# Retention head 0: score products moved behind the fifth of the seven value/gate products, and half of one product sum moved to the other transposition bank

## The chip, the cores and the metric

The kernel runs on one core of one Trainium2 chip, as a single launch. The metric is the device time in microseconds (us), the median of three executions. Beside it there is one profiled execution, whose trace gives the start and length of every instruction on each engine: PE (TensorE, matrix products and transposes), DVE (VectorE), ACT (ScalarE), POOL (GpSimd), SP (the engine that issues most of the loads) and the DMA queues. Each engine runs its instructions strictly in the order in which they stand in its own list; between engines they wait for one another by semaphores.

## What is computed

A two-layer encoder on 512 tokens of width 1024, float32. Layer one is latent attention beside a pooling mixer; it is not touched. Layer two is bidirectional retention with four heads (query and key width 256, value width 512). Cut to what matters:

```python
h = rms_norm(x, norm_g)
q, k, v, gate = jnp.split(h @ w_in, [RET_QK, 2 * RET_QK, 2 * RET_QK + RET_V], axis=-1)
q = apply_rope(q.reshape(B_, T, RET_HEADS, RET_DK), cos_r, sin_r)
k = apply_rope(k.reshape(B_, T, RET_HEADS, RET_DK), cos_r, sin_r) * (RET_DK ** -0.5)
o = o_f + o_b            # retention forward and backward: (q k^T * decay) v, all 512 x 512 pairs here
o = (o - mu) * lax.rsqrt(var + NORM_EPS) * gn_g     # norm per head
y = o * jax.nn.silu(gate)
x = x + y @ w_out
```

The kernel holds the 512 x 512 decay factors of a head as shifted views of one table `gp` and so computes each head in one pass: scores, times decay, times values.

## The kernel before

**Arithmetic.** Every float32 operand is split in a high part (rounded for the fast matmul, a CAST on ACT, names ending in H) and a low remainder (a subtraction on DVE, names ending in L). A product of two such operands is three matmuls: H with H, L with H, H with L. In `mm3` these are lines 72, 75 and 76, in the products of `vg` lines 792, 794 and 795. One matmul is 128 x 128 against 128 x 512.

**Head 0 of layer two, in program order.** `qk_gemm` and `rope_pair` make q and k (rotation: lines 768 to 773 on DVE, split: lines 81 and 82). The inverse norms of the tokens come from a small chain: `ss2` on DVE (line 1005), scale and epsilon on DVE (line 175), a power on POOL (line 177), then three small copies on DVE (lines 1006 to 1008: `r2`, `nr2`, `r2s`). `decay(h)` fills `gp` (lines 731 and 732 on DVE, an exponential on ACT, line 733). `r_scores` makes four 128 x 512 score tiles in PSUM, six matmuls each, two buffers named `sc`; each is scaled and multiplied by the decay on DVE (line 864) and split (lines 81 and 82). `vg` makes the values and the gate. `r_head_out` then multiplies scores by values (48 matmuls), multiplies by the gate and turns the result with PE transposes into the two PSUM buffers named `tr` (`turn`, line 877).

**The seven products of `vg`.** Values and gates of a head are one 2 x 2 block product, done in Strassen's way with seven products of half size instead of eight. In order they are A11, S1, S4, S2, S3, A12, A22, 24 matmuls each (two weight tiles i = 0, 1, each for two token halves p = 0, 1). They are summed in PSUM in three pairs of tiles, X, Z and Y, one tile for each half p: A11 and A12 go to X, S1 and S4 to Z, S2, S3 and A22 to Y. Before a later product may add to a pair, DVE has read the intermediate sum: line 826 reads Z after S1, lines 835 and 836 read Y after S2 and Z after S4, line 842 reads Y after S3, line 851 after A22. ACT copies X after A11 to SBUF (line 821, `p1`), which lines 826, 835 and 851 add.

**Weights.** A weight tile is 128 x 1024. ACT casts it (line 784, `wH`, four buffers), DVE subtracts (line 785, `wL`, three buffers). Raw tiles arrive in four `raw` buffers by SP loads (line 682) of 512 KB. The pair `t3` for S3 is a load followed by an adding DMA issued from POOL (line 684) to the same buffer; POOL's power of line 177 stands ahead of the two adding DMAs in POOL's list. The pair `b21` is loaded to the two `raw` buffers in which `b22` lies, so each of its loads waits until DVE has made the `wL` of that `b22` tile (product S4). Line 829 adds `b22` and line 839 adds `b21` to the pair `tt`, which is the weight of S1, then of S2, then of A22.

**What sets the order.** A scheduler of the language layer reorders the instructions of each engine when the program is built, except where one is held in program order (`keep_in_program_order`, which `mm3` takes as its `pin`). So the order on an engine isn't the text's, but it is fixed before the run.

Of the kernel before, what the change touches and what calls it, by code (L numbers as in the profile page):

```python
# [37 lines left out]
def trunk(ctx: ExitStack, tc: tile.TileContext, x, positions, a_norm_g, a_w_in, a_q_norm_g, a_w_uq,  # L38
# [11 lines left out]
    def S(tag, shape=(P, T), dt=F32):  # L50
        count[0] += 1
        return sb.tile(list(shape), dt, tag=tag, name=f"{tag}_{count[0]}", bufs=BUFS[tag])
# [4 lines left out]
    def PS(tag):  # L57
        count[0] += 1
        return ps.tile([P, T], F32, tag=tag, name=f"{tag}_{count[0]}", bufs=PBUFS[tag])

    mm = nc.tensor.matmul
# [6 lines left out]
    def f(ap):  # L68
        return ap.bitcast(F32)

    def mm3(pt, lH, lL, rH, rL, st, sp, pin=False):
        i = mm(pt, lhsT=lH, rhs=rH, start=st, stop=False)  # L72
        if pin:
            tc.keep_in_program_order(i)
        mm(pt, lhsT=lH, rhs=rL, start=False, stop=False)  # L75
        mm(pt, lhsT=lL, rhs=rH, start=False, stop=sp)  # L76

    def split(src, tag):
        h = S(tag, dt=F32R)
        l = S(tag, dt=F32R)  # L80
        nc.scalar.copy(h, src)
        V.tensor_sub(l, src, f(h))
        return h, l
# [255 lines left out]
    ss = S("sm", (P, 4))  # L339
# [166 lines left out]
    def values(g4):  # L506
        uH, uL = wunit(ukv[:, g4 * 4:(g4 + 1) * 4, 128:256], 4, P)
        uH = uH.rearrange("p a b -> p (a b)")
        uL = uL.rearrange("p a b -> p (a b)")
        vH, vL = [], []  # L510
        for t in range(4):
            pt = PS("mm")
            tk = slice(t * P, (t + 1) * P)
            mm3(pt, kvH[:, tk], kvL[:, tk], uH, uL, True, True)
            h, l = split(pt, "V")
            vH.append(h)
            vL.append(l)
        return vH, vL
# [79 lines left out]
    vv = values(0)  # L598
# [5 lines left out]
    for h in range(8):  # L604
# [3 lines left out]
        if h == 4:  # L608
            vv = values(1)
# [65 lines left out]
    def vg_src(h, r, c, i):  # L675
        c0 = 4096 - c * 2048 + h * T
        return wv[:, r, 2 * i:2 * i + 2, c0:c0 + T]
# [9 lines left out]
    def first_sums(h, then=lambda i: i):  # L687
        return [load("tw", vg_src(h, 0, 0, i), vg_src(h, 0, 1, i), then=then) for i in range(2)]

    tt0 = first_sums(0, pin)  # L690
# [38 lines left out]
    def decay(h):  # L729
        e = gp.rearrange("p a b -> p (a b)")[:, :E]  # L730
        V.tensor_scalar(out=e, in0=idx, scalar1=nlb[:, 4 + h:5 + h], scalar2=1.0, op0=ALU.mult, op1=ALU.mult)
        V.scalar_tensor_tensor(out=e, in0=idx, scalar=lg[:, h:h + 1], in1=e, op0=ALU.mult, op1=ALU.min)
        act(e, e, AF.Exp)
        return [e[:, (3 - j) * P:(3 - j) * P + T] for j in range(4)]
# [38 lines left out]
        V.tensor_add(c, c, d)  # L773
        return split(a, tag), split(c, tag)

    def vg(h, tt=None):

        tags = dict(X=("mm", "mm"), Z=("mm", "tr"), Y=("mm", "sc"))
        ps_ = {n: [PS(t) for t in tt] for n, tt in tags.items()}

        def product(name, a, ws, first):
            for i in range(2):
                wh, wl = S("wH", (P, 1024), F32R), S("wL", (P, 1024), F32R)
                nc.scalar.copy(wh, ws[i])  # L784
                V.tensor_sub(wl, ws[i], f(wh))  # L785
                last = i == 1
                for p in range(2):
                    o = ps_[a][p]
                    for k2 in range(2):
                        c = slice(k2 * T, (k2 + 1) * T)  # L790
                        lh, ll = (x[:, p * P:(p + 1) * P] for x in forms[2 * i + k2][name])
                        mm(o, lhsT=lh, rhs=wh[:, c], start=first and i == 0 and k2 == 0, stop=False,  # L792
                           skip_group_check=True)
                        mm(o, lhsT=lh, rhs=wl[:, c], start=False, stop=False, skip_group_check=True)  # L794
                        mm(o, lhsT=ll, rhs=wh[:, c], start=False, stop=last and k2 == 1, skip_group_check=True)  # L795

        vv = [None] * 4
        gs = [None] * 4

        def value(t, src):  # L800
            sm = S("sm", (P, 4))
            act(src, src, AF.Copy, scale=nr2[:, t:t + 1], accum_out=sm[:, 0:1])
            V.tensor_scalar(out=sm[:, 1:2], in0=sm[:, 0:1], scalar1=-1.0 / T, scalar2=1.0, op0=ALU.mult, op1=ALU.mult)
            hh = S("V", dt=F32R)
            ll = S("V", dt=F32R)
            act(hh, src, AF.Identity, bias=sm[:, 1:2])
            V.scalar_tensor_tensor(out=ll, in0=src, scalar=sm[:, 1:2], in1=f(hh), op0=ALU.add, op1=ALU.subtract)
            vv[t] = (hh, ll)

        rng = range(2)  # L810

        def src(r, c, i):
            return vg_src(h, r, c, i)

        b11 = [load("raw", src(0, 0, i)) for i in rng]
        if tt is None:
            tt = first_sums(h)
        product("A11", "X", b11, True)
        p1 = [S("t") for _ in rng]
        for p in rng:  # L820
            nc.scalar.copy(p1[p], ps_["X"][p])
        b22 = [load("raw", src(1, 1, i)) for i in rng]
        product("S1", "Z", tt, True)
        v = [S("t") for _ in rng]
        for p in rng:
            V.tensor_add(v[p], ps_["Z"][p], p1[p])
        t3 = [load("raw", src(0, 1, i), src(1, 1, i), then=pin) for i in rng]
        for i in rng:
            V.tensor_add(tt[i], tt[i], b22[i])
        product("S4", "Z", b22, False)  # L830
        b21 = [load("raw", src(1, 0, i)) for i in rng]
        product("S2", "Y", tt, True)
        u2 = [S("t") for _ in rng]
        for p in rng:
            V.tensor_add(u2[p], ps_["Y"][p], p1[p])
            V.tensor_add(u2[p], ps_["Z"][p], u2[p])
            value(p, u2[p])
        for i in rng:
            V.tensor_add(tt[i], tt[i], b21[i])
        product("S3", "Y", t3, False)  # L840
        for p in rng:
            V.tensor_add(v[p], ps_["Y"][p], v[p])
            value(2 + p, v[p])
        product("A12", "X", b21, False)
        for p in rng:
            gs[p] = S("l1")
            act(gs[p], ps_["X"][p], AF.Silu, scale=r2[:, p:p + 1])
        product("A22", "Y", tt, False)
        for p in rng:
            c = S("l1")  # L850
            V.tensor_add(c, ps_["Y"][p], p1[p])
            act(c, c, AF.Silu, scale=r2[:, 2 + p:3 + p])
            gs[2 + p] = c
        return vv, gs

    def r_scores(q, k, ds, tag):
        ss = []
        for j in range(4):
            tk = slice(j * P, (j + 1) * P)
            pt = PS("sc")  # L860
            for i in range(2):
                mm3(pt, k[i][0][:, tk], k[i][1][:, tk], q[i][0], q[i][1], i == 0, i == 1)
            s = S("t")
            V.scalar_tensor_tensor(out=s, in0=pt, scalar=r2s[:, j:j + 1], in1=ds[j], op0=ALU.mult, op1=ALU.mult)
            ss.append(split(s, tag))
        return ss
# [116 lines left out]
    for h in range(4):  # L983
        A, B = ("qk", "y") if h % 2 == 0 else ("y", "qk")
        if h == 0:
            res = [residual(0), residual(1)]
            next(res[0])
            pq = qk_gemm(0, 1)
            sums_of_halves(0)
            sums_of_halves(1)  # L990
            next(res[0])
            pq += qk_gemm(P, 1)
            pk = qk_gemm(1024, 1)
            sums_of_halves(2)
            sums_of_halves(3)
            next(res[1])
            next(res[1])
        else:
            pq = qk_gemm(h * 256, then=pend[2])
            pk = qk_gemm(1024 + h * 256, 1)  # L1000
            rs = out_scale(pend[1])
        q = rope_pair(pq, A)
        k = rope_pair(pk + qk_gemm(1024 + h * 256 + P, 1), A)
        if h == 0:
            V.tensor_add(ss2[:, 0:4], ss2[:, 0:4], ss2[:, 4:8])
            V.tensor_copy(r2, pow_mhalf(ss2[:, 0:4], 1.0 / DM))
            V.tensor_scalar(out=nr2, in0=r2, scalar1=-1.0, scalar2=1.0, op0=ALU.mult, op1=ALU.mult)
            V.tensor_scalar(out=r2s, in0=r2, scalar1=0.0625, scalar2=1.0, op0=ALU.mult, op1=ALU.mult)
        else:
            r_out(h - 1, pend[0], rs)  # L1010
        ss = r_scores(q, k, decay(h), B)
        vv, gs = vg(h, tt0 if h == 0 else None)
        pend = r_head_out(ss, vv, gs, A)
    for i in range(2):
        gt = S("y" if A == "qk" else "qk")
# [47 lines left out]
```

## Time and profile before

| | |
|---|---|
| runs | 792.81 us median of 3 (792.67, 792.81, 794.54) |
| profiled execution | 794.41 us, of which 792.6 us span from first to last instruction |
| PE busy | 781.1 us, 99% of the span, mean granted clock 0.998 |
| DVE busy | 579.0 us (73%) |
| ACT busy | 403.4 us (51%) |
| POOL busy | 38.6 us (5%) |
| DMA | 80.91 MB, mean 102 GB/s |

The "span" is the time between the first and the last instruction of the profiled execution. A row of the timeline has the start, the length, the engine, the line, the operation, the tiles written and read, and in square brackets how long the engine had been idle just before and who released it. A matmul row's length is its whole passage through the array; matmuls that don't wait start 0.227 us apart although each is shown as 0.39 us long. In head 0 the products lie between 403 and 451 us.

### The profile page before, as it was taken

How to read it: one execution, taken by the hardware profiler on the slowest of the kernel's cores; microseconds unless marked ns; L12 is line 12 of the kernel's file. 1: busy time of each engine (PE TensorE's matmuls, PEld its weight loads, DVE VectorE, ACT ScalarE, POOL GpSimd, SP SyncE). 2: the span in 40 equal slices, each digit the busy share in tenths (PEclk: the TensorE clock that was granted, in tenths of full speed). 3: DMA queues.
4: the chain of work that ended last, by engine and by line, in shares of the span. 5: the costliest groups of instructions: out<-in, count | busy, mean ns of one | idle time of the engine just before them, and what ended most of it. 6: DMA issues, size and time to landing. Idle time of an engine off the chain costs nothing. (4 is left out here: it accounts for less than half of the span.)

```text
span 792.6 us, 9592 instructions
## 1 busy us (share of the span) xinstructions
PE 781.1 (99%) x3546; PEld 642.0 (81%) x3546; DVE 579.0 (73%) x938; ACT 403.4 (51%) x670; POOL 38.6 (5%) x60
## 2 busy tenths in 40 slices
PE   9999999999999999999999999999999999999996
PEld 7888888888888888888877888888888888888885
DVE  4689986768748677899679747787377884767845
ACT  6645346666626744318654832358333583334832
POOL 0010000000000000100010100100101001010003
PEclk9999999999999999999999999999999999999999
DMA  8722233132123312353315822447324373244202
GB/s 254 226 62 83 70 82 87 39 80 91 54 72 88 103 38 69 87 152 107 107 37 133 227 56 80 111 111 210 74 79 110 103 203 84 71 122 102 85 27 108
DMA packets 87832, 80.91 MB, mean 102 GB/s; under 512 B 7868, under 2 KB 67304, under 8 KB 87784
## 3 DMA queue, kind: packets, MB, share of 16 engines
q1 hardware_dynamic: 82984, 71.11, 29.8%
q0 software_dynamic: 4352, 8.39, 7.0%
q10 hardware_dynamic: 448, 0.79, 0.3%
q8 instruction: 28, 0.46, 0.2%
q14 instruction: 20, 0.16, 0.1%
HBM read 76.87 MB, written 2.10 MB: 100 GB/s over the span
## 5 line engine op out<-in xcount | busy, mean ns | idle before, releaser
L72 PE MATMUL mm<-hT,wH 128*128 128x512 f32 x352 | 139.0, 395 | 0.3 <-ACT wH L281 0.3
L75 PE MATMUL mm<-hT,wH 128*128 128x512 f32 x352 | 137.8, 392 | 0.0
L76 PE MATMUL mm<-hT,wL 128*128 128x512 f32 x352 | 137.8, 392 | 0.0
L108 ACT CAST wH<-raw 128x1024 fp32r<-128x1024 f32 (+3 forms) x77 | 70.7, 923 | 114.4 <-PE mm L75 91.3
L109 DVE TENSOR_TENSOR wL<-raw,wH 128x1024 fp32r<-128x1024 f32 (+3 forms) x77 | 81.4, 1059 | 13.1 <-issue 4.7
L72 PEld LDWEIGHTS mm<-hT,wH 128*128 128x128 f32 x352 | 66.5, 189 | 14.0 <-ACT wH L281 0.7
L76 PEld LDWEIGHTS mm<-hT,wL 128*128 128x128 f32 x352 | 66.5, 189 | 14.0 <-DVE wL L282 0.2
L75 PEld LDWEIGHTS mm<-hT,wH 128*128 128x128 f32 x352 | 66.5, 189 | 13.6
L784 ACT CAST wH<-raw 128x1024 fp32r<-128x1024 f32 x32 | 33.7, 1054 | 50.2 <-PE mm L76 20.2
L785 DVE TENSOR_TENSOR wL<-raw,wH 128x1024 fp32r<-128x1024 f32 x32 | 38.9, 1220 | 10.4 <-issue 7.2
L784 ACT CAST wH<-tw 128x1024 fp32r<-128x1024 f32 x24 | 25.1, 1047 | 40.9 <-PE mm L76 26.3
L904 ACT ACTIVATE wH<-raw,cols 128x512 fp32r<-128x512 f32 x32 | 21.4, 717 | 43.8 <-issue 32.8
L925 DVE SCALAR_TENSOR_TENSOR xT<-mm,sm,xT 128x512 f32<-128x512 f32 (+1 forms) x33 | 24.1, 731 | 25.1 <-PE mm L76 25.0
L75 PE MATMUL mm<-y,wH 128*128 128x512 f32 x96 | 37.2, 389 | 0.0
L76 PE MATMUL mm<-y,wL 128*128 128x512 f32 x96 | 37.2, 389 | 0.0
L72 PE MATMUL mm<-y,wH 128*128 128x512 f32 x96 | 37.2, 390 | 0.0
L785 DVE TENSOR_TENSOR wL<-tw,wH 128x1024 fp32r<-128x1024 f32 x24 | 29.3, 1220 | 2.8 <-PE tr L794 1.0
L794 PE MATMUL mm<-wL,hT 128*128 128x512 f32 x80 | 31.1, 389 | 0.0
L795 PE MATMUL mm<-wH,hT 128*128 128x512 f32 x80 | 31.1, 389 | 0.0
L792 PE MATMUL mm<-wH,hT 128*128 128x512 f32 x80 | 31.0, 389 | 0.0
L885 DVE TENSOR_TENSOR l<-mm,l 128x512 f32<-128x512 f32 x16 | 11.1, 692 | 23.9 <-PE mm L76 23.9
L504 DVE TENSOR_TENSOR xT<-mm,xT 128x512 f32<-128x512 f32 x24 | 16.4, 688 | 15.0 <-PE mm L76 14.8
(361 smaller groups left out, 1903.6 us busy)
## 6 DMA issues: line engine op xcount, KB each, us to landing
raw<-in_r_w_in_dram SPq DMA_DIRECT2D x48, 512.0 KB, 3.7
raw<-in_a_w_in_dram SPq DMA_DIRECT2D x25, 512.0 KB, 4.0
raw<-in_a_w_out_dram SPq DMA_DIRECT2D x16, 512.0 KB, 3.9
raw<-in_r_w_out_dram SPq DMA_DIRECT2D x16, 512.0 KB, 5.5
tw<-in_r_w_in_dram SPq DMA_DIRECT2D x8, 512.0 KB, 3.8
tw<-in_r_w_in_dram POOLq DMA_DIRECT2D x8, 512.0 KB, 6.6
raw<-in_r_w_in_dram POOLq DMA_DIRECT2D x8, 512.0 KB, 6.0
l<-in_x_dram SPq DMA_DIRECT2D x8, 256.0 KB, 4.7
```

The source lines that it names most:

```text
L72: i = mm(pt, lhsT=lH, rhs=rH, start=st, stop=False)
L75: mm(pt, lhsT=lH, rhs=rL, start=False, stop=False)
L76: mm(pt, lhsT=lL, rhs=rH, start=False, stop=sp)
L108: then(nc.scalar.copy(h[:, c], raw[:, c]))
L109: then(V.tensor_sub(l[:, c], raw[:, c], f(h[:, c])))
L784: nc.scalar.copy(wh, ws[i])
L785: V.tensor_sub(wl, ws[i], f(wh))
L792: mm(o, lhsT=lh, rhs=wh[:, c], start=first and i == 0 and k2 == 0, stop=False, skip_group_check=True)
L794: mm(o, lhsT=lh, rhs=wl[:, c], start=False, stop=False, skip_group_check=True)
L795: mm(o, lhsT=ll, rhs=wh[:, c], start=False, stop=last and k2 == 1, skip_group_check=True)
L904: act(wh[:, c], raw[:, c], AF.Copy, scale=g)
L925: V.scalar_tensor_tensor(out=a, in0=pt[:, :T // n], scalar=rs[:, t:t + 1], in1=a, op0=ALU.mult, op1=ALU.add)
```

## The change

For head 0 alone, `r_scores` is no longer called ahead of `vg` but by `vg` itself, behind S3 and its two value tiles and ahead of A12; `decay(0)` is called there too. For all four heads the second tile of the pair Y is taken from the `tr` buffers instead of the `sc` buffers. The very first score matmul of each head is held in program order.

```diff
-    def vg(h, tt=None):
-
-        tags = dict(X=("mm", "mm"), Z=("mm", "tr"), Y=("mm", "sc"))
+    def vg(h, tt=None, mid=None):
+
+        tags = dict(X=("mm", "mm"), Z=("mm", "tr"), Y=("mm", "tr"))
         ps_ = {n: [PS(t) for t in tt] for n, tt in tags.items()}
...
             V.tensor_add(v[p], ps_["Y"][p], v[p])
             value(2 + p, v[p])
+        if mid:
+            mid()
         product("A12", "X", b21, False)
...
-                mm3(pt, k[i][0][:, tk], k[i][1][:, tk], q[i][0], q[i][1], i == 0, i == 1)
+                mm3(pt, k[i][0][:, tk], k[i][1][:, tk], q[i][0], q[i][1], i == 0, i == 1, i == 0 and j == 0)
...
-        ss = r_scores(q, k, decay(h), B)
-        vv, gs = vg(h, tt0 if h == 0 else None)
+        if h == 0:
+            ss = []
+            vv, gs = vg(h, tt0, lambda: ss.extend(r_scores(q, k, decay(0), B)))
+        else:
+            ss = r_scores(q, k, decay(h), B)
+            vv, gs = vg(h)
```

What the scheduler makes of it shows in the order of the instructions. In its rows a tile's name carries a running number, and the numbers of the same tile differ between the two kernels: Z is `mm_3919` and `tr_3920` before and `mm_3864` and `tr_3865` now; the line numbers of the changed file are 2 higher behind line 843.

PE, at the start of S1, before (`qk_3797` and `qk_3798` are q, `qk_3846` is k, `sc` tiles are scores):

```order
L795 MATMUL mm_3918<-wH_3943,hT_3528 128x512
L792 MATMUL mm_3919<-wH_3967,pt_3611 128x512
L792 MATMUL tr_3920<-wH_3967,pt_3611 128x512
L72 MATMUL sc_3865<-qk_3797,qk_3846 128x512
L75 MATMUL sc_3865<-qk_3798,qk_3846 128x512
L72 MATMUL sc_3878<-qk_3797,qk_3846 128x512
L75 MATMUL sc_3878<-qk_3798,qk_3846 128x512
L794 MATMUL mm_3919<-wL_3968,pt_3611 128x512
L795 MATMUL mm_3919<-wH_3967,pt_3612 128x512
L792 MATMUL mm_3919<-wH_3967,pt_3629 128x512
```

The same place now:

```order
L795 MATMUL mm_3863<-wH_3888,hT_3528 128x512
L792 MATMUL mm_3864<-wH_3912,pt_3611 128x512
L792 MATMUL tr_3865<-wH_3912,pt_3611 128x512
L794 MATMUL mm_3864<-wL_3913,pt_3611 128x512
L795 MATMUL mm_3864<-wH_3912,pt_3612 128x512
L792 MATMUL mm_3864<-wH_3912,pt_3629 128x512
```

Before, all 24 score matmuls stood inside S1, 12 in the half of each weight tile; now S1's matmuls follow each other, and the first that needs a `wL` stands directly behind the two that don't. The scores now stand behind S3: 12, then 3 of A12, then 12.

ACT, over the same stretch, before (`t_3959` and `t_3960` are `p1`, the copies of X):

```order
L784 CAST wH_4011<-raw_3963 128x1024
L784 CAST wH_4027<-raw_3965 128x1024
L81 CAST qk_3846<-t_3836 128x512
L81 CAST qk_3850<-t_3838 128x512
L784 CAST wH_4047<-tw_3375 128x1024
```

and now:

```order
L784 CAST wH_3956<-raw_3908 128x1024
L821 COPY t_3904<-mm_3862 128x512
L821 COPY t_3905<-mm_3863 128x512
L784 CAST wH_3972<-raw_3910 128x1024
L81 CAST qk_3846<-t_3836 128x512
L81 CAST qk_3850<-t_3838 128x512
L784 CAST wH_3992<-tw_3375 128x1024
```

The two copies of X have moved from behind the score splits to a place ahead of the second `b22` cast and the splits of k.

DVE, from the reads of Z after S1 to the read of Y after S2, before (`tw` is `tt`; `wL_4102` and `wL_4118` are the two tiles of `t3` for S3):

```order
L785 TENSOR_TENSOR wL_4064<-tw_3378,wH_4063 128x1024
L731 TENSOR_SCALAR gp<-l_783_3371,nlb 128x896
L839 TENSOR_TENSOR tw_3375<-tw_3375,raw_4043 128x1024
L839 TENSOR_TENSOR tw_3378<-tw_3378,raw_4045 128x1024
L785 TENSOR_TENSOR wL_4102<-raw_4003,wH_4101 128x1024
L785 TENSOR_TENSOR wL_4118<-raw_4006,wH_4117 128x1024
L732 SCALAR_TENSOR_TENSOR gp<-l_783_3371,lg,gp 128x896
L835 TENSOR_TENSOR t_4079<-mm_3921,t_3959 128x512
```

and now:

```order
L785 TENSOR_TENSOR wL_3957<-raw_3908,wH_3956 128x1024
L785 TENSOR_TENSOR wL_3973<-raw_3910,wH_3972 128x1024
L785 TENSOR_TENSOR wL_3993<-tw_3375,wH_3992 128x1024
L785 TENSOR_TENSOR wL_4009<-tw_3378,wH_4008 128x1024
L839 TENSOR_TENSOR tw_3375<-tw_3375,raw_3988 128x1024
L785 TENSOR_TENSOR wL_4047<-raw_3948,wH_4046 128x1024
L839 TENSOR_TENSOR tw_3378<-tw_3378,raw_3990 128x1024
L785 TENSOR_TENSOR wL_4063<-raw_3951,wH_4062 128x1024
L835 TENSOR_TENSOR t_4024<-mm_3866,t_3904 128x512
```

The four score multiplications and their four splits, and the two lines of head 1's decay, are gone from here to behind S3; both additions of `b21` and both `wL` of `t3` still stand ahead of the first read of Y. Two loads of activation tables are new on ACT, around head 1's exponential, which now stands between the gate's first and second pair of SiLUs. The lists of SP and POOL are the same as before, and from head 1 on only the buffer name of Y's second tile differs.

## Prediction

> **What bounds the kernel now.** I read the page's engine table first, then the busy time of the engines by stretch, then PE's timeline in head 0's products.
>
> ```profile
> span 792.6 us, 9592 instructions
> PE 781.1 (99%) x3546; PEld 642.0 (81%) x3546; DVE 579.0 (73%) x938; ACT 403.4 (51%) x670; POOL 38.6 (5%) x60
> ...
> 409.00:424.00 15.00, 12.46 (x52) 9.49 (x52) 13.91 (x23) 7.04 (x11) 3.81 (x3) 1.00 0.45 67
> 424.00:435.00 11.00, 10.54 (x47) 8.35 (x46) 10.18 (x11) 3.85 (x4) 0.00 (x0) 1.00 0.47 143
> ```
>
> PE is the bound of the whole. The two stretches (length, then busy us of PE, PEld, DVE, ACT, POOL) are an exception: PE has gaps, and DVE is 93% busy in both, so here DVE paces PE. The timeline of PE has the gaps in place.
>
> ```profile
> 403.06 0.39 PE L792 MATMUL mm<-wH,hT 128*128 128x512 f32 x1
> ...
> 408.73 0.39 PE L792 MATMUL tr<-wH,pt 128*128 128x512 f32 x1
> 410.32 0.50 PE L72 MATMUL sc<-qk,qk 128*128 128x512 f32 x1 [1.20 <-ACT qk L81]
> 410.66 0.39 PE L75 MATMUL sc<-qk,qk 128*128 128x512 f32 x1
> ...
> 421.45 0.45 PE L792 MATMUL mm<-wH,l 128*128 128x512 f32 x1
> 422.61 0.49 PE L792 MATMUL tr<-wH,l 128*128 128x512 f32 x1 [0.71 <-DVE t L826]
> 423.74 0.50 PE L794 MATMUL mm<-wL,l 128*128 128x512 f32 x1 [0.64 <-DVE wL L785]
> 434.94 0.50 PE L792 MATMUL mm<-wH,l 128*128 128x512 f32 x1 [0.46 <-DVE t L835]
> 450.96 0.39 PE L72 MATMUL mm<-V,y 128*128 128x512 f32 x1
> ```
>
> The four waits in brackets are 3.0 us together; a change that neither adds nor removes a matmul can win little more than these. From 403.06 to 408.73 are 25 steps, 0.227 us each; after a wait the first step is 0.34 (410.32 to 410.66), 0.11 lost again.
>
> **The equal-time point.** The row at 434.94 is the first matmul of S3; 450.96 is the first of `r_head_out`. Before, 70 matmuls lie from the one to the other; now it is 96, the 24 scores and 2 of A12 more. With 0.227 a step and 0.11 for the restart, S3 would have to begin at 450.96 - 0.11 - 96 x 0.227 = 429.1 for the same time. The change is therefore worth (start of S3) - 429.1, if nothing waits behind it.
>
> **PE's own way to S3.** These rows carry it.
>
> ```profile
> 408.70 1.05 ACT L784 CAST wH<-raw 128x1024 fp32r<-128x1024 f32 x1 [1.66 <-PE mm L795]
> 409.66 1.14 ACT L81 CAST qk<-t 128x512 fp32r<-128x512 f32 x2
> ...
> 419.45 1.07 ACT L821 COPY t<-mm 128x512 f32<-128x512 f32 x2
> 408.92 1.22 DVE L785 TENSOR_TENSOR wL<-tw,wH 128x1024 fp32r<-128x1024 f32 x1
> 410.30 0.69 DVE L82 TENSOR_TENSOR qk<-t,qk 128x512 fp32r<-128x512 f32 x1 [0.16 <-ACT qk L81]
> ...
> 412.60 0.17 DVE L1006 COPY r<-sm 128x4 f32<-128x4 f32 x1 [0.93 <-POOL sm L177]
> 412.67 1.23 DVE L785 TENSOR_TENSOR wL<-tw,wH 128x1024 fp32r<-128x1024 f32 x1
> ...
> 421.87 0.68 DVE L826 TENSOR_TENSOR t<-tr,t 128x512 f32<-128x512 f32 x1
> 422.47 2.35 DVE L785 TENSOR_TENSOR wL<-raw,wH 128x1024 fp32r<-128x1024 f32 x2
> ```
>
> *First wait.* The scores no longer stand at 408.96, but the first L794 of S1 does, and its `wL` is made from 408.92 to 410.14. PE starts 0.06 behind a DVE end (422.55, 422.61): 410.20, 1.24 lost where 1.36 was. The wait changes its name only.
>
> *Second wait, new.* The copies of X now stand ahead of the second cast on ACT. The second needs A11's last matmul, which released the cast at 408.70; so copy 408.70, cast 409.23, split of k 410.19 instead of 409.66: 0.53 later, and with it, through L82, the norm's chain and POOL's power, everything from 412.60 on DVE. The second `wL` of S1 ends at 412.67 + 0.53 + 1.23 = 414.43. PE, with no scores between, wants it at 410.20 + 0.34 + 10 x 0.227 = 412.81: 1.68 lost. Queued behind it are S1's rest and all later products.
>
> *S4.* DVE steps on by 1.14 for a 1024 wide row (the x2 row), 0.60 for a 512 wide one (421.87 to 422.47) and 0.07 for a small one (412.60 to 412.67): two small copies, two L829, two L826, the second ending at 418.04, then the first `wL` of S4, ending at 419.18. PE wants S4's second matmul at 417.78 and, after 0.227, its first L794: it loses 0.32 and 0.90, where 0.93 (421.45 to 422.61) and 0.90 (to 423.74) were. The eight score operations are no longer in DVE's way, but PE lacks the 5.4 us of score matmuls too.
>
> Together, with a restart of 0.11 behind each of three, 1.24 + 1.68 + 0.32 + 0.90 + 0.33 = 4.5 us are lost, against 3.5 up to here before (1.36 + 0.93 + 0.90 + 0.33). From 408.73, 70 matmuls: PE reaches S3 at 408.96 + 15.9 + 4.5 = 429.3.
>
> **DVE's and the DMAs' way to S3.** S3's first matmul waits for L835, and ahead of that stand the two L839 and both `wL` of `t3`.
>
> ```profile
> 411.16 1.40 POOL L177 TENSOR_TENSOR sm<-sm,mhalf 128x4 f32<-128x4 f32 x1 [72.41 <-DVE sm L175]
> 412.53 1.23 POOL L684 DMA_DIRECT2D raw<-in_r_w_in_dram  x1
> 418.89 1.22 POOL L684 DMA_DIRECT2D raw<-in_r_w_in_dram  x1 [5.13 <-issue]
> 423.76 1.52 SPq L682 DMA_DIRECT2D raw<-in_r_w_in_dram  x2
> DMA to landing us min/median/max: 6.0/6.0/6.0
> ...
> DMA to landing us min/median/max: 8.6/8.6/8.6
> DMA to landing us min/median/max: 9.0/9.0/9.0
> ...
> DMA to landing us min/median/max: 6.1/6.3/7.8
> ```
>
> The first landing line is POOL's adding DMAs at 410 to 420 us, alone on the DMA engines; the next two are POOL's at 545.7 and 645.5, while SP's loads run; the last is SP's loads in the former's company. Before, the second adding DMA (418.89 to 424.9) was over when SP issued the loads of `b21` (423.76, 0.07 behind the first `wL` of S4, and one `wL` later). Now that `wL` is done at 419.18, so SP issues at 419.25 and 420.38, and POOL's DMA, late by the 0.53 of the power, at 419.42. They collide. By the collision's rows the adding DMA lands at 419.42 + 8.6 to 9.0 = 428.0 to 428.4, the second load at 420.38 + 6.1 to 7.8 = 426.5 to 428.2. Behind the adding DMA come its cast (1.05), its `wL` (1.14 to the next on DVE), L835 (0.68) and two handovers (0.08): S3 at 431.0 to 431.4. The load's own way (L839 1.14, `wL` 1.14, L835 0.74) ends no later. So S3 begins 1.9 to 2.3 us behind the equal-time point, 2.1 in the middle, and PE, there since 429.3, waits.
>
> A rule of the Trainium skill bears on this (DMA: Bandwidth & Descriptors, "Queues, rings and completion order"): each DMA engine goes round between the queues that have work, packet by packet. If instead the older request were served first, the adding DMA would keep its 6.0 and land at 425.4; the sum would then be set by PE's own way, +0.2. The trace agrees with the rule: 8.6 and 9.0 against 6.0.
>
> **Behind S3.** Scores: 24 matmuls, four multiplications, four casts and four subtractions move; they issue no DMA. The multiplications take
>
> ```profile
> L864 DVE SCALAR_TENSOR_TENSOR t<-sc,r2s,gp x16: 739/743/749, 415.1 to 714.0; 128x512 f32<-128x512 f32 x16
> ```
>
> 0.74 each. DVE's next `wL` needs the buffer that S3's last L794 gives back, 22 steps and 0.39 after S3's start, 5.5 us; behind it come that `wL` (1.14), a value step of the same kind as L864 (0.66 to the next), a small one (0.07), the read of Y (0.60) and the first score multiplication (0.74): 8.7 and a handover, 8.8. PE wants that score buffer again 39 matmuls after S3's start, at 9.0. Hidden, with 0.15 to spare; if the cover goes, each 0.1 of slip costs 0.1, at most one 0.74. Head 1's decay and two more table loads on ACT:
>
> ```profile
> 445.02 1.28 ACT L847 ACT_TABLE_LOAD   x1
> 452.14 0.68 DVE L851 TENSOR_TENSOR l<-sc,t 128x512 f32<-128x512 f32 x1
> 459.62 0.60 PE L877 MATMUL tr<-ident,l 128*128 128x128 f32 x4
> 459.82 0.69 DVE L885 TENSOR_TENSOR l<-mm,l 128x512 f32<-128x512 f32 x1 [1.46 <-PE mm L76]
> ```
>
> 2 x 1.28 on ACT ahead of the second pair of SiLUs, whose first reader is the L885 at 459.82: nothing, with some 4 us of cover; without it 2.6 at most. The Y tile in a `tr` buffer: its last read is the L851 at 452.14, the next writer of that buffer the turn at 459.62: nothing, here and in the other heads, whose order is the same. Between 0 and 0.7 in all; I take 0.
>
> **Sum.** +2.1 us. On the profiled execution's own time, 794.41 (1.8 around its 792.6 span), that is 796.5; the median of the runs is 1.6 lower, 792.81, and gives 794.9, 0.26% more. What a measurement here tells from no change is about 0.3%, 2.4 us, so this is "no change", but close to its edge.
>
> **Rivals.** *Slower: the adding DMA is starved.* Before, DVE's second addition of `b21` started when its load had landed:
>
> ```profile
> 429.73 1.23 DVE L839 TENSOR_TENSOR tw<-tw,raw 128x1024 f32<-128x1024 f32 x1 [0.59 <-DMA raw<-in_r_w_in_dram]
> ```
>
> If `b21` goes first (before, 6.0 us from SP's issue at 423.76 until L839 could start at 429.73; now to 425.2) and the adding DMA's 6.0 less its 1.23 of issue follows, it lands at 430.0; halfway between that and the forecast's 428.4 is 429.2, S3 at 432.2, +3.1 us, 795.9. It decides from a landing later than 428.5, 9.1 us after its issue: then the loss passes 2.4. For it: 9.0 has been seen. Against: 8.6 too, and there as much load traffic ran beside it.
>
> *No collision that matters.* The adding DMA lands by 426.3, as in 6.0 to 6.9 us; then PE's own way counts, 429.3, +0.2 us, 793.0. For it: the first of the two loads has the engines to itself for its first 1.2 us or so, until POOL's packets come. Against: the three transfers start within 1.2 us of each other.
>
> *Faster: DVE's relief pays out.* DVE loses the eight score operations in the stretch, 4 x (0.66 + 0.60) = 5.0 us, PE its 5.4; in the rows before DVE was the later of the two. If all waits but the first (1.35 with its restart) went, 4.2 - 1.35 = 2.9 us would be won, 789.9. It needs the second `wL` of S1 1.7 us earlier than worked out, and the power of 1.40 us on POOL stands before it.
>
> *The clock drops.* PE would now stand still three times for 1.2 to 1.9 us.
>
> ```profile
> 6.95 0.80 PE L72 MATMUL mm<-hT,wH 128*128 128x512 f32 x1 [0.32 <-ACT wH L281]
> ...
> 10.53 0.39 PE L76 MATMUL mm<-hT,wL 128*128 128x512 f32 x1
> ```
>
> At the kernel's start 8 matmuls took 3.58 us instead of 1.82; one such stretch costs 1.8 us more, +3.9, 796.7. Against: before, waits of 1.20 and of 0.71 and 0.64 in close order left the granted clock at 1.00. The Trainium skill (TensorE: Matmul & The Clock Gate, "Why this matters for your kernels") warns of idle gaps above about 3 us; none here is so long.
>
> **Numbers.** Forecast 0.45, starved 0.28, no collision 0.20, clock 0.04, faster 0.03. The forecast's upper end lies at the bound, so a fifth of it counts as slower: slower 0.41, same 0.56, faster 0.03. The range goes from below the no-collision case (792.6) to the clock's case and the worst landing (796.7); the forecast's own is 794.3 to 795.5.
>
> **What the new trace would show.** A wait of about 1.2 us for S1's first `wL` and of 1.6 for its second, released by DVE L785; SP's loads of `b21` issued near 419.3 and 420.4; POOL's second adding DMA landing 8 to 9 us after issue; then PE idle some 1.7 us at S3's first L792, released by L835; none of size at the scores. I am wrong if `b21` or the adding DMA land early, if the scores wait for their buffers, or if a matmul step anywhere behind 409 us is 0.43.

## The result and the profile after

The changed kernel took 798.41 us (median of 6 runs, 796.68 to 799.17) against 793.94 (6 runs, 792.67 to 795.17): a ratio of 1.0052, 95% interval 1.0039 to 1.0065. It is 4.5 us slower, where 2.1 were forecast (794.9, from 792.6 to 796.7). The forecast stood on 792.81 for the kernel before; its median over six runs is 1.1 higher, so 1.1 of the 3.5 us between 794.9 and 798.41 is not the change. The profiled execution of the changed kernel took 796.9 us, 1.5 less than the median; why is told with the second group of experiments.

The engine table of the changed kernel's page:

```profile
span 795.1 us, 9592 instructions
PE 780.0 (98%) x3546; PEld 640.7 (81%) x3546; DVE 579.5 (73%) x938; ACT 406.3 (51%) x672; POOL 38.6 (5%) x60
```

TensorE is busy for 1.1 us less and idle for longer. Its waits, largest first (what waited, for what, us in total, times, longest):

```profile
PE mm L792 <- DVE t L835: 3.4, 1, 3.4
PE mm L794 <- DVE wL L785: 3.1, 3, 1.4
```

Before, the wait for L835 was 0.46 us and those for L72, L826 and `wL` were 1.20, 0.71 and 0.64. The scores now wait for nothing. The places of the waits on TensorE's timeline, from the first S1 matmul on the `tr` tile (408.73 before, 407.39 here: this execution got through the kernel's start 1.34 us sooner, mostly because the product at 7 us ran at about 0.23 us a step and not at the half clock of the prediction's rows, so its times are to be read 1.34 later against the prediction's) to the first of `r_head_out`:

```profile
407.39 0.39 PE L792 MATMUL tr<-wH,pt 128*128 128x512 f32 x1
408.85 0.50 PE L794 MATMUL mm<-wL,pt 128*128 128x512 f32 x1 [1.08 <-DVE wL L785]
413.10 0.50 PE L794 MATMUL mm<-wL,pt 128*128 128x512 f32 x1 [1.43 <-DVE wL L785]
417.84 0.50 PE L794 MATMUL mm<-wL,l 128*128 128x512 f32 x1 [0.64 <-DVE wL L785]
427.72 0.39 PE L795 MATMUL tr<-wH,pt 128*128 128x512 f32 x1
431.49 0.47 PE L792 MATMUL mm<-wH,l 128*128 128x512 f32 x1 [3.38 <-DVE t L835]
453.44 0.39 PE L72 MATMUL mm<-V,y 128*128 128x512 f32 x1
```

From the first row to the last are 46.05 us; before, from 408.73 to 450.96, 42.23. That is 3.82 us more for the same matmuls. S3's first matmul, the row at 431.49, stands 24.10 us behind the first row, and the equal-time point stood at 20.4 (429.1 - 408.73): 3.7 of the 3.82 are lost by then, most of them in the 3.38 us ahead of this row. VectorE, POOL and SP show what it waited for:

```profile
422.19 1.23 DVE L839 TENSOR_TENSOR tw<-tw,raw 128x1024 f32<-128x1024 f32 x1 [0.70 <-DMA raw<-in_r_w_in_dram]
423.33 1.22 DVE L785 TENSOR_TENSOR wL<-raw,wH 128x1024 fp32r<-128x1024 f32 x1
428.38 1.23 DVE L839 TENSOR_TENSOR tw<-tw,raw 128x1024 f32<-128x1024 f32 x1 [3.83 <-DMA raw<-in_r_w_in_dram]
429.52 1.22 DVE L785 TENSOR_TENSOR wL<-raw,wH 128x1024 fp32r<-128x1024 f32 x1
430.66 0.69 DVE L835 TENSOR_TENSOR t<-mm,t 128x512 f32<-128x512 f32 x1
...
411.67 1.23 POOL L684 DMA_DIRECT2D raw<-in_r_w_in_dram  x1
418.09 1.22 POOL L684 DMA_DIRECT2D raw<-in_r_w_in_dram  x1 [5.18 <-issue]
417.86 1.52 SPq L682 DMA_DIRECT2D raw<-in_r_w_in_dram  x2
424.58 0.37 SPq L100 DMA_DIRECT2D raw<-in_r_w_in_dram  x1
```

SP issues the two loads of `b21` within 1.2 us, the first of them 0.2 us ahead of POOL's second adding DMA. That first load is there for VectorE 4.3 us after its issue (422.19). VectorE then stands still for 3.83 us, until the second load has landed, with the addition, a `wL` and L835 in line behind it, 3.0 us of work that TensorE sits out. The adding DMA's own time from issue to landing was 6.0 us alone before; here it is

```profile
DMA to landing us min/median/max: 10.0/10.0/10.0
```

and VectorE could start on the second load, issued near 419.0, 9.4 us later. The two ways end almost together: the cast of the adding DMA's tile starts on ACT at 428.21 and ends near 429.3, and its `wL` starts at 429.52. The row at 424.58 was not in the sum: head 1's first weight load, which SP now also issues while these are in flight.

### The profile page after: what moved, and what is told of

Read it like the earlier page. It is cut to its first block, busy times and chain, and to the rows that moved or that the text cites. A ratio compares the mean times of both kernels' runs of the same rounds, so it can differ in the third digit from the quotient of the medians.

```text
span 795.1 us, 9592 instructions
## 1 busy us (share of the span) xinstructions
PE 780.0 (98%) x3546; PEld 640.7 (81%) x3546; DVE 579.5 (73%) x938; ACT 406.3 (51%) x672; POOL 38.6 (5%) x60
## 4 chain that ended last, share of the span: by engine, by line
PE 84%; issue 11%; DVE 3%; DMA 1%; POOL 1%; ACT 0%; POOLq 0%; DVEq 0%; SPq 0%
PE mm L72 18%; PE mm L76 18%; PE mm L75 18%; PE mm L792 4%; PE mm L795 4%; PE mm L794 4%; PE tr L792 2%; PE tr L795 2%; PE tr L794 2%; PE sc L72 2%; PE sc L75 2%; PE sc L76 2%; PE tr L575 2%; DMA raw<-in_r_w_in_dram 1%; PE sc L557 1%
## 5 line engine op out<-in xcount | busy, mean ns | idle before, releaser
L72 PE MATMUL mm<-hT,wH 128*128 128x512 f32 x352 | 138.2, 393 | 0.3 <-ACT wH L281 0.3
L72 PEld LDWEIGHTS mm<-hT,wH 128*128 128x128 f32 x352 | 66.1, 188 | 14.0 <-ACT wH L281 0.7
L785 DVE TENSOR_TENSOR wL<-raw,wH 128x1024 fp32r<-128x1024 f32 x32 | 39.0, 1222 | 10.4 <-issue 7.2
L72 PE MATMUL mm<-y,wH 128*128 128x512 f32 x96 | 37.2, 390 | 0.0
```

## Experiments

**First group: where does the wait come from?** The theory was the prediction's collision, harder than priced; the rivals were the moved tile of Y, and a wait that has nothing to do with the DMAs. The first kernel is the change once more.

> The changed kernel once more, beside the others on one chip. Collision theory: +3.8 us of waits in head 0 against before, 3.4 us of it one wait at S3's first matmul. Clock theory: some executions carry a second slow stretch of the clock and show 0.996 instead of 0.998 as the mean clock, 1.7 us longer; about half of them or more, so ratio 1.004 to 1.006. If the clock readings are chance and have nothing to do with the wait, before and the other kernels of this call show 0.996 just as often.

It took 798.92 us against 793.76 (ratio 1.0073, 1.0055 to 1.0092), above the expected 1.004 to 1.006; all six executions had the low clock. The waits were the same but for a longer one at S3 (3.75 us; the adding DMA took 10.4), and behind that wait this execution shows something that the changed kernel's profile had not:

```profile
432.00 0.47 PE L792 MATMUL mm<-wH,l 128*128 128x512 f32 x1 [3.75 <-DVE t L835]
432.31 0.39 PE L794 MATMUL mm<-wL,l 128*128 128x512 f32 x1
...
433.12 0.63 PE L794 MATMUL mm<-wL,l 128*128 128x512 f32 x1
433.55 0.63 PE L795 MATMUL mm<-wH,l 128*128 128x512 f32 x1
...
436.41 0.39 PE L792 MATMUL mm<-wH,l 128*128 128x512 f32 x1
```

From 433.12 the matmuls start 0.43 us apart instead of 0.227, and at 436.41 the usual step is back. More on that below.

Y's second tile in the `tr` bank alone, with the scores where they were:

```
-        tags = dict(X=("mm", "mm"), Z=("mm", "tr"), Y=("mm", "sc"))
+        tags = dict(X=("mm", "mm"), Z=("mm", "tr"), Y=("mm", "tr"))
```

> The kernel before with only the second tile of the sum Y in a transposition bank; the scores stay where they were. Collision theory: the bank is free long before it is wanted, so 0.0 us, ratio 0.999 to 1.001, clock 0.998. Rival, the bank costs by itself (a turn that waits for the last read of Y, in each of four heads): about +1 us a head, ratio 1.004 to 1.005.

Measured 794.17 us, ratio 1.0004 (0.9992 to 1.0016); the wait at S3 is 0.4 us, as before, and from the first S1 matmul on the `tr` tile to `r_head_out` are 42.22 us (42.23 before). The bank costs nothing, so the loss belongs to the order.

The change, with the second of the two adding DMAs left out in the first head:

```
-        t3 = [load("raw", src(0, 1, i), src(1, 1, i), then=pin) for i in rng]
+        t3 = [load("raw", src(0, 1, i), *([] if h == 0 and i == 1 else [src(1, 1, i)]), then=pin) for i in rng]
```

> The change, but in head 0 the second adding DMA of the pair t3 is left out (that half of the weight of S3 lacks a summand). Collision theory: the two loads of b21 are alone on the DMA engines and land 3.7 and 4.9 us after issue, S3 does not wait (under 0.3 us), ratio 1.000 to 1.001, all executions at clock 0.998. Rival, the order on DVE alone (both additions of b21 and both subtractions of t3 ahead of the read of Y): the wait at S3 stays at 2 us or more and the ratio at 1.003 or more.

Measured 793.48 us, ratio 1.0006 (0.9992 to 1.0020). TensorE's waits in it:

```profile
PE mm L794 <- DVE wL L785: 3.2, 3, 1.5
PE sc L160 <- POOL t L157: 1.3, 1, 1.3
PE mm L72 <- ACT wH L281: 0.8, 1, 0.8
```

The three waits for `wL` stand as in the change, the one at S3 is gone, and with it all of the loss, although both additions of `b21` and both `wL` of `t3` still stand ahead of the read of Y. The rest of the reordering is worth +0.2 us (42.41 from the first row to `r_head_out`, against 42.23), as the prediction's case without a collision had it. That all executions would have a clock of 0.998 did not come true: 4 of 12 had 0.994 to 0.996, and were 2.4 us and more longer than the rest.

The change, with the adding DMAs out of the loads' way: the chain of the token norms is written behind them, so that POOL does not stand at its power before it issues. `token_norm` holds the four lines of `ss2`, `r2`, `nr2` and `r2s`, taken out of the loop over heads.

```
+    def token_norm():
...
         t3 = [load("raw", src(0, 1, i), src(1, 1, i), then=pin) for i in rng]
+        if h == 0:
+            token_norm()
```

> The change, but the small chain for the token norm (with the power on POOL) stands behind the two adding DMAs of t3 in the program. POOL can then issue the adding DMAs as soon as the first loads have landed, near 398 and 404 us, so they are over before the loads of b21 start, and the second subtraction for S1 no longer waits for the power. Collision theory: no wait at S3, the second wait in S1 (1.4 us in the change) gone, the first (1.1 us) stays; worked out to S3 starting 0.9 us ahead of the equal-time point, ratio 0.998 to 1.000, clock 0.998. Rival, order on DVE: S3 still waits 2 us or more, ratio 1.003 or more.

Measured 792.38 us, ratio 0.9986 (0.9975 to 0.9998). Lines from 776 on are 6 to 8 higher in this kernel. POOL's issues on the timeline:

```profile
396.25 1.21 POOL L684 DMA_DIRECT2D raw<-in_r_w_in_dram  x1 [58.66 <-DVE wL L791]
405.30 1.22 POOL L684 DMA_DIRECT2D raw<-in_r_w_in_dram  x1 [7.84 <-DVE qk L82]
```

TensorE's waits:

```profile
PE mm L800 <- DVE wL L791: 1.7, 2, 1.0
PE sc L160 <- POOL t L157: 1.3, 1, 1.3
```

The second adding DMA now starts at 405.30 and lands in 6.2 us; `b21` is loaded from 416.82, alone; S3 waits for nothing. The new second wait (1.4) is gone too. Both kernels that keep the DMAs apart lose the wait: the collision is its cause.

**Which transfers collide?** Head 1's load at 424.58 had been left out of the sum. It was to be held back by one more tile of the `raw` ring.

```
         b21 = [load("raw", src(1, 0, i)) for i in rng]
+        if h == 0:
+            G.memset(S("raw", (P, 1024))[:, 0:1], 0.0)
```

> The change, with one more tile of the `raw` ring taken by a one-column memset on POOL behind b21's loads, so that the load of head 1's first weight tile waits for the splits of t3's second tile and no longer runs beside b21's loads and the adding DMA. If the third load is what made the landings late (the sum left it out): the adding DMA lands at most 9.2 us after its issue (10.0 in the changed kernel), b21's second load at most 8.2 (9.4), the wait at S3 falls to 1.5 to 2.5 us (3.4), the clock stretch goes with it, and the time is 794.5 to 796.0 us. Rival, b21's two loads do it alone: the adding DMA still takes 9.6 or more, S3 waits 3.2 us or more, the time is 797.5 to 799.0.

This failed as a test: the memset was over at 424.40, the ring gave its tile to the load at once, and SP issued it at 424.43, as in the change. It took 799.23 us (ratio 1.0075), one more repeat. With a second write to that tile, by VectorE behind S2's sums, the hold is real:

```
+        if h == 0:
+            hold = S("raw", (P, 1024))[:, 0:1]
+            G.memset(hold, 0.0)
...
             value(p, u2[p])
+        if h == 0:
+            V.tensor_copy(hold, u2[1][:, 0:1])
```

> The change, with a tile of the `raw` ring taken by a one-column memset on POOL behind b21's loads and written once more by VectorE behind the sums of S2, so that head 1's first weight load can't start until then (about 431 instead of 424.5). This time the load is really held. If that third load made the landings late: the adding DMA lands at most 9.2 us after its issue (10.0 to 10.3 in the changed kernel), b21's second load at most 8.2 (9.4), the wait at S3 is 1.5 to 2.5 us, no stretch at half clock, 794.0 to 795.8 us. Rival, b21's two loads do it alone: the adding DMA takes 9.6 or more, S3 waits 3.2 us or more, 797.5 to 799.2.

SP's issues in it, and S3's first matmul:

```profile
419.86 1.52 SPq L682 DMA_DIRECT2D raw<-in_r_w_in_dram  x2
432.72 0.37 SPq L100 DMA_DIRECT2D raw<-in_r_w_in_dram  x1
...
433.44 0.47 PE L792 MATMUL mm<-wH,l 128*128 128x512 f32 x1 [3.30 <-DVE t L838]
```

POOL's adding DMA, issued at 420.02:

```profile
DMA to landing us min/median/max: 10.0/10.0/10.0
```

The third load starts at 432.72, behind it all, and the adding DMA still takes 10.0 us and S3 still waits 3.30. So `b21`'s second load (9.3 here) and the adding DMA are as late without the third load; the load missing from the sum cost nothing. The time was 800.53 us, ratio 1.0083 (1.0055 to 1.0111), above even the rival's range; the profiled execution (800.44) came 2.0 us later to the first S1 matmul on the `tr` tile than the changed kernel's, of which more below.

**Second group: does the wait drop the clock?** Of the 12 executions of the change, 2 had a mean granted clock of 0.998 (796.68 and 796.90 us, one of them the profiled one) and 10 had 0.994 to 0.996 (797.97 to 801.29). Of 29 of the kernel before, 5 were at 0.995 or 0.996, and of the 34 of the three kernels above without the wait, 11 were at 0.994 to 0.996, so the wait is not the only thing that lowers it. The theory: a TensorE idle for so long is given half the clock for a while. The rival: the low clock goes with the crowded DMAs, or comes by chance. The test makes the wait without the DMAs, on the kernel with the norm moved, by n idle reads of Y's first tile on VectorE:

```
         u2 = [S("t") for _ in rng]
+        for i in range(n if h == 0 else 0):
+            V.scalar_tensor_tensor(out=v[0], in0=ps_["Y"][0], scalar=0.0, in1=v[0], op0=ALU.mult, op1=ALU.add)
```

> Base: the kernel with the norm behind the adding DMAs (e3_norm_behind_adds: 792.4 us, no wait at S3). Ahead of VectorE's reads of Y behind S2, two more reads of Y's first tile (first head only; they add zero times Y to v). No DMA is changed. Worked out from that kernel's rows (a dependent 128x512 step each 0.73 us, VectorE's read starting at 425.75 and TensorE's S3 due at 427.0): TensorE waits 1.0 us at S3. Both theories: about +1.0 us, 793.0 to 794.0, no stretch at half clock.

> As with two reads, with four, and one weight split that the scheduler puts between them: TensorE waits 3.5 us at S3, as in the changed kernel, but with no late DMA. If the wait itself drops the clock: a stretch at half clock behind S3's start in most executions, clock 0.994 to 0.996 in most runs, and 3.5 + 1.5 us over the base: 796.7 to 798.0. If the low clock came with the crowded DMAs or by chance: clock as the base (0.997 to 0.999 in 8 of 11), and 3.5 us over it: 795.4 to 796.4.

> As with two reads, with seven, and two weight splits between them: TensorE waits 6.9 us at S3. If the wait itself drops the clock: every execution has the stretch at half clock of about 3.4 us, and the time is 6.9 + 1.6 us over the base: 800.4 to 801.6. If not: clock as the base, 798.8 to 799.8.

All three missed the wait they were built for. The scheduler saw the delay and put matmuls of A12 ahead of S3, so TensorE waited at most 1.0 us anywhere there; with four reads (us in total, times, longest):

```profile
PE mm L800 <- DVE wL L791: 2.5, 3, 1.0
```

The times were 793.14, 793.99 and 796.36 us (ratios 0.9997, 1.0004 and 1.0033; the first inside its range, but with a wait of 0.3 us at S3 instead of 1.0), and with seven reads the granted clock was 0.997 to 0.999 in all six runs. They say nothing on long waits, but the profiled execution with two reads tells where a low mean can come from: its 0.996 is a stretch at half clock from 7.6 to 11.0 us, at the kernel's start, and no other until the kernel's last microseconds. With the matmuls of S2, S3 and A12 kept in the order written, the wait comes:

```
+            one = pin if h == 0 and name in ("S2", "S3", "A12") else lambda i: i
...
-                        mm(o, lhsT=lh, rhs=wl[:, c], start=False, stop=False, skip_group_check=True)
+                        one(mm(o, lhsT=lh, rhs=wl[:, c], start=False, stop=False, skip_group_check=True))
```

> Base e3_norm_behind_adds (no wait at S3); four reads more of Y's first tile by VectorE ahead of its sums behind S2, and the matmuls of S2, S3 and A12 kept in the order written, so that TensorE can't take other work first. No DMA is changed. From the base's rows: 4 x 0.73 us and one weight split of 1.15 between them make TensorE wait 3.5 us at S3. If such a wait drops the clock: a stretch at half clock behind it, clock 0.994 to 0.996 in most runs, 796.7 to 798.0. If the low clock comes with the crowded DMAs or by chance: clock as the base (mostly 0.997 to 0.999), 795.2 to 796.4.

> As with four reads, with seven: TensorE waits 5.7 us at S3. If such a wait drops the clock: the stretch at half clock in every execution, 799.0 to 800.4. If not: 797.4 to 798.6 and the clock as the base.

With four reads 799.41 us, ratio 1.0070 (1.0054 to 1.0086); with seven 804.08, ratio 1.0129 (1.0108 to 1.0151). Both are above the theory's ranges, by 1.4 and 3.7 us. Four reads, the wait and the steps behind it (lines are 7 to 11 higher than in the changed kernel):

```profile
432.55 0.47 PE L799 MATMUL mm<-wH,l 128*128 128x512 f32 x1 [3.30 <-DVE t L846]
...
434.52 0.63 PE L801 MATMUL tr<-wL,l 128*128 128x512 f32 x1
434.95 0.63 PE L802 MATMUL tr<-wH,l 128*128 128x512 f32 x1
```

TensorE in the same kernel by stretch (window, length and busy us, instructions, granted clock, share and rate of the DMAs):

```profile
428.00:432.00 4.00, 1.25 (x6) 1.00 0.51 147
432.00:436.00 4.00, 3.45 (x11) 0.74 0.40 115
436.00:440.00 4.00, 4.00 (x17) 0.83 0.23 66
```

Seven reads, a wait of 5.5 us:

```profile
428.00:432.00 4.00, 2.21 (x10) 1.00 0.71 209
432.00:436.00 4.00, 0.31 (x1) 0.58 0.44 131
436.00:440.00 4.00, 4.00 (x11) 0.57 0.00 0
```

And the change's own profile, the one execution with a wait of this length and no drop:

```profile
428.00:432.00 4.00, 0.62 (x3) 1.00 0.08 24
432.00:436.00 4.00, 4.00 (x19) 1.00 0.65 183
```

With seven reads, no DMA runs at all from 436 to 440 us, in the midst of the half clock, and in neither kernel does TensorE wait for one; in the kernel with the memset alone the clock fell at 431.3 us, with the DMAs idle since 430.0. A wait of 3.3 us brings it without the collision. It is not certain at that length: 3.30 brought it in two kernels, 3.67 and 3.75 brought it, 3.38 in the changed kernel's profile did not; the last section shows what told them apart. The stretch costs 0.20 us in each of seven or eight matmuls, 1.5 us. With seven reads all six runs were at 0.990 to 0.994; with four, three were at 0.992 to 0.996 and three at 0.997, the profiled one, which has the stretch, among the latter: the mean over a whole execution is a weak sign of 1.5 us.

What the pinned kernels lost beyond their ranges lies, in their profiled executions (799.49 and 802.86 us), ahead of anything that was edited. From the first S1 matmul on the `tr` tile to `r_head_out` these took 46.87 and 49.29 us, against 41.30 in their base: 5.6 and 8.0 more, the upper ends of what the theory's ranges leave over the base (4.3 to 5.6 and 6.6 to 8.0). The fixed order's other wait, 0.93 us ahead of S4, is in this. But the end of the wait for S1's first `wL` stood at 410.57 and 411.52, against 408.83 in the base: 1.7 and 2.7 us later. These are lost in the first 13 us. With four reads the matmuls from 7.80 to 10.36 us stand 0.43 us apart, in the base 0.23; the clock column shows 1.00 there, because the trace's record of the clock begins only at 10.7 us. With seven reads the first of these matmuls started 1.1 us later than in the base, and the clock was at half from 9.4 to 12.8 us; in the kernel with the held load it was from 7.8 to 11.2 us. What decides on the clock in the kernel's start stays open. So a low mean clock does not say which of the two places it comes from.

**A better version.** The kernel with the norm moved still waits 1.0 us for S1's first `wL`, which stands on VectorE behind k's rotation. Written ahead of the rotation's two last sums, it should come 1.2 us sooner: for k in head 0, `rest` is called behind the split of S1's first tile.

```
-        V.tensor_sub(a, a, b)
-        V.tensor_add(c, c, d)
-        return split(a, tag), split(c, tag)
+        def rest():
+            V.tensor_sub(a, a, b)
+            V.tensor_add(c, c, d)
+            return split(a, tag), split(c, tag)
...
```

> Base e3_norm_behind_adds; the last two sums of k's rotation in the first head, and the splits of them, written behind the split of S1's first tile, so that VectorE does that split 1.2 us earlier. If the first wait (1.15 us and a restart of 0.11) goes and nothing takes its place: 791.0 to 791.6 us, ratio to the kernel before 0.996 to 0.998. Rival, the wait moves to S1's second split or to S4: as the base, 0.998 to 0.999.

Measured 793.10 us, ratio 0.9990 (0.9978 to 1.0001): the rival. Its longest wait in head 0 (lines 4 to 6 higher than in the base):

```profile
PE mm L806 <- DVE wL L795: 1.6, 1, 1.6
```

The wait at S1 went, and the one at S4 grew from 0.7 to 1.6: VectorE has as much to do up to there as before. The two are not told apart (0.9990 and 0.9986). The kernel with the norm moved is 0.14% under the kernel before, which is less than the 0.3% that a measurement here tells from nothing.

## Why the prediction was wrong, step by step

**Right.** The way of TensorE to S3: waits of 1.24, 1.68, 0.32 and 0.90 us were worked out and 1.23, 1.60, 0.29 and 0.90 were lost, so the split of k, the norm's chain and POOL's power did shift as told. The issues: the loads of `b21` at 419.25 were to come 10.52 us behind 408.73 and came 10.47 behind 407.39; the adding DMA 10.69, and came 10.70. S3 to `r_head_out`: 0.11 + 96 x 0.227 = 21.9, measured 21.95, so nothing waited behind S3; from there to the end are 341.7 us in both kernels, so the table loads and the bank cost nothing. Without the collision the change is worth +0.2, as that rival said; the run without the second adding DMA showed it.

**Wrong, the first term: the landings.** "By the collision's rows the adding DMA lands at 419.42 + 8.6 to 9.0 ..., the second load at 420.38 + 6.1 to 7.8." It was 10.0 and 9.4. The rows came from later heads, where the loads beside the adding DMA began about 1 us ahead of it and 1 us and more behind it; here all three start within 1.2 us, the first load just ahead. The second load's way then ended last, 428.38 + 1.14 + 1.14 + 0.7 = 431.4, and S3 began 24.1 us behind the first row instead of 22.3 to 22.7: 1.4 to 1.8 us more, which takes the forecast's 1.9 to 2.3 to 3.7. The rival of a starved adding DMA put the landing at 429.2 to 430.0; in the prediction's clock it was 429.4. Its direction was right, and its chance of 0.28 too low, because two values from another place had been taken as the bounds. Its picture, that `b21` goes first and the adding DMA starves behind it, was half right: the first load was hardly late (4.3 us until VectorE had it, 3.8 without the second adding DMA), but the second came as late as the adding DMA. The Trainium skill (DMA: Bandwidth & Descriptors, "Queues, rings and completion order") has each DMA engine going round between queues with work; 10.0 and 9.4, instead of 6.0 alone and a median of 3.7 for such loads in the profile before, agree with that. What such a meeting costs was measured here, not derived.

**Wrong, the second term: the clock.** The rival had 0.04, with the words that no wait was near 3 us; that hung on the first term. With S3's wait at 3.4 to 3.75 us instead of 1.7, an execution can pay some 1.5 us on top; of the profiled ones of the change, of the change with the memset and of the change with the held load, three of four did. The warning of the Trainium skill (TensorE: Matmul & The Clock Gate, "Why this matters for your kernels") about idle gaps above about 3 us is borne out by four of five executions with 3.3 to 3.75 us. The stretch is much as the one at the kernel's start, 0.43 us a step against 3.58 us for 8, and the rival's price of 1.8 for it was close to the 1.5 measured.

**The sum.** The lost steps are +3.8 us. The mean clock was low in 10 of 12 executions; if each of these paid 1.5 us for a stretch behind S3, the mean is 3.8 + 1.25 = 5.1, against a difference of medians of 4.5 in one set and 5.2 in the other. That count is an inference: only two of the twelve were profiled, one with the stretch and one without, and a low mean can also come from the kernel's start. The forecast named these two as separate rivals of 3.1 and 3.9 us and never added them; its upper end, 796.7, was the larger of the two alone.

## What to carry to other kernels

When a change lets a load start sooner, look at what is in flight at that moment, and price a collision by more than the worst row of another place: here two of three transfers of 512 KB, which take 6.0 us and less alone, took 9.4 and 10.0, and VectorE, which runs its list in order, stood behind the last of them. A wait that grows past 3 us on TensorE should be priced with a chance of a stretch at half clock behind it, and rivals that feed each other belong in one sum. Here taking a slow POOL operation out of the adding DMAs' way kept them apart, and the order of the products then cost nothing.

## What the runs showed of the hardware that was not expected

The half clock does not begin at a fixed time behind the start of the wait. Read in steps of half a microsecond, the granted clock fell 2.4 us (seven reads), 3.3 (the memset alone), 4.4 (held load), 4.6 (the repeat of the change) and 4.7 us (four reads) after TensorE's last matmul had ended. In the first two it fell while TensorE still waited; in the other three TensorE had started again and run three to five matmuls at full speed, so a look at the restart alone would have shown nothing.

What fixes the time is a grid. In each of these traces' records of the clock, all changes lie a whole number of times 3.413 us apart: the stretch at half clock is one such window long in four executions and two, 6.8 us, with seven reads. The repeat of the change in two windows of its grid, the last at full clock and the one at half (window, length and busy us, instructions, granted clock, share and rate of the DMAs):

```profile
429.43:432.84 3.41, 0.84 (x4) 1.00 0.09 25
432.84:436.25 3.41, 3.41 (x10) 0.50 0.65 187
```

The five windows at whose end the clock fell had TensorE busy for a share of 0.03, 0.25 (the row above), 0.29, 0.31 and 0.40. Of all other windows at full clock that lie between 401 and 459 us, in the 14 profiled executions, none had less than 0.49. That fits the idle of 3.38 us that passed: in the changed kernel's own grid a window ended in the middle of it, and the two that share it were half busy:

```profile
426.43:429.84 3.41, 1.68 (x8) 1.00 0.48 140
429.84:433.25 3.41, 1.76 (x8) 1.00 0.37 103
```

So where a wait of this length falls in the grid would decide whether it costs 1.5 us. This is read from five falls; no run shifted a wait against the grid.
